# Second-half u made on ScalarE, channels paired per bank, and four mixing products taken channel by channel, at the end of a first feed-forward block

## The chip, the core and the metric

The kernel runs on one core of a Trainium2 chip. The core has a matrix engine (TensorE, PE in the profile; its weight loads are PEld), a vector engine (VectorE, DVE), an activation engine (ScalarE, ACT), GpSimd (POOL) and a queue engine that issues most transfers (SyncE, SP). Results of PE land in eight accumulator banks of PSUM, 2 KB per partition each, which DVE and ACT read; everything else lies in SBUF. The metric is the device time of one execution in microseconds; lower is better.

## The reference, cut to what matters

One transformer layer over 512 tokens of 1024 channels in float32: a modulated feed-forward block, a mixer of two branches (a chunked mLSTM and a forgetting attention), and a second feed-forward block.

```python
def hybrid_layer(x, c, ...):
    u = rms_norm(x, ffn1_norm_g) * (1 + sc1) + sh1
    x = x + 0.5 * g1 * swiglu(u, ffn1_w_in, ffn1_w_out)

    u = rms_norm(x, mix_norm_g) * (1 + sc2) + sh2        # the u of this text
    z = u @ w_mix + b_mix
    q_m, k_m, v_m, o_m, i_m, f_m, q_f, k_f, v_f, f_f, g_a, g_b = ...   # slices of z
    qk_m = silu(causal_conv(concatenate([q_m, k_m]), conv_w, conv_b))
    ...                                                   # mLSTM, attention, gates
    x = x + g2 * (merged @ w_out)
    u = rms_norm(x, ffn2_norm_g) * (1 + sc3) + sh3
    x = x + 0.5 * g3 * swiglu(u, ffn2_w_in, ffn2_w_out)
    return x
```

The change lies where `x` of the first block is complete, the second `u` is formed, and the first 512 columns of `z` (`q_m`, in four blocks of 128 columns) are computed.

## The kernel before, in words

Every float32 matrix product is made of three products of rounded parts. An operand `w` is split into a high part `wh` (ACT, line 96) and a remainder `wl` (DVE, line 98), and PE adds high by high (line 115), high by remainder and remainder by high (lines 116 and 117). Activations `u` are kept transposed: eight tiles of 128 channels by 512 tokens, each as a high part `uh[k]` and a remainder `ul[k]`.

`u_from` makes one channel tile for one half of the tokens (256 columns) out of a transposed piece in a bank: ACT writes `uh` (line 250: scale and shift in one pass), a second pass writes the unrounded `uf`, and a subtraction gives `ul` (line 255). The second pass is on DVE (line 254) unless `start` is set, in which case it is on ACT (line 252). The subtraction is on POOL for odd channels and on DVE for even ones; with `start` set, it is always on DVE.

`norm_turn` transposes the normalised tokens on PE (line 271) into four banks `b` and calls `u_from` for each channel. Before the change channel k and channel k + 4 share bank k % 4, and the sixteen transposes run through the channels in order, so a bank is complete only when its channel k + 4 is in.

In `run`, the first feed-forward block ends with `pair_out`. The first token half of `u` is made while that still runs. Then come the normalisation of the second half (`norm_scale`), the weights of the four `q_m` blocks (`ws`), the four products over the first 256 tokens into four banks `pp`, the transposes and `u` of the second half, and then the four products over the last 256 tokens (`gemm_stat`, block by block, each over its eight channels). After these follow the causal convolution of the four blocks (`qk_conv`), a narrow product for the gate columns (`gates`, 96 columns, weights `rawg`), and four more blocks, m = 4 to 7, which are `k_m`.

The order of the work is not just that of the text. The build places each engine's instructions in a list of its own, going by its own estimate of when inputs are ready, and then adds the waits between engines. In the kernel before it has mixed the products of the first two blocks with one another. Three kinds of buffer tie the places together:

- split weights `wh` and `wl`: four buffers each. The four `q_m` blocks hold all of them, so the gate weights can be split only when the first block's last product is done;
- raw weights `raw`: three buffers, in turn, the gate weights' `rawg` among them. The load for block 6 takes the buffer of `rawg` and waits for its split on DVE (line 98);
- banks `g`: four. The gate product takes the bank of the first `q_m` block, which ACT must have read (`cz`, line 956).

In `qk_conv` ACT copies the bank to `cz`, DVE does four multiply-adds into `cy` (lines 958 and 960), ACT applies silu (961) and rounds (964), and DVE takes the remainder `qkl` (965). In `gates` DVE adds the bias (`gz`, 922), ACT does three functions (923 to 925), for which it loads another function table twice, and DVE goes on (926 onward).

Of the kernel before, what the change touches and what calls it, by code (L numbers as in the profile page):

```python
# [20 lines left out]
P = 128  # L21
# [3 lines left out]
NK = 8  # L25
# [23 lines left out]
class Layer:  # L49
# [213 lines left out]
            self.u_tiles()  # L263
        return self.xnorm(hf, pool)

    def norm_turn(self, hf, xn, G, sh, b, ks=range(NK)):

        nc = self.nc
        for k in range(NK):
            for i in range(2):  # L270
                nc.tensor.transpose(b[k % 4][:, k // 4 * 256 + i * P:k // 4 * 256 + (i + 1) * P],
                                    xn[i][k // 4][:, k % 4 * P:(k % 4 + 1) * P], self.ident)
        u = lambda k: self.u_from(b[k % 4][:, k // 4 * 256:(k // 4 + 1) * 256], k, hf * 256, 256, G[:, k:k + 1], sh[:, k:k + 1], self.tp)
        for k in ks:
            u(k)
        return u

    def gemm_stat(self, ps, w, c0, c1, ks=range(NK)):
        wh, wl = w
        for k in ks:  # L280
            self.mm3(ps[:wh.shape[2], c0:c1], wh[:, k, :], wl[:, k, :],
                     self.uh[k][:, c0:c1], self.ul[k][:, c0:c1], k == 0, k == NK - 1)
# [178 lines left out]
    def product(self, ps, A, W, first, tail=0, hooks={}):  # L461

        chunks = [(c, min(2, NP - c)) for c in range(0, NP, 2)]
        def run(t, part, ops):
            ah, al, wh, wl = ops
            mm = self.nc.tensor.matmul
            c, n = part
            for k in range(n):
                s = slice(t * P, (t + 1) * P)
                a = (ah(c + k)[:, s], al(c + k)[:, s])  # L470
                end = c + k == NP - 1
                mm(ps[t], a[0], wh[:, k, :], start=first and c + k == 0, stop=False, skip_group_check=True)  # L472
                mm(ps[t], a[0], wl[:, k, :], start=False, stop=False, skip_group_check=True)  # L473
                mm(ps[t], a[1], wh[:, k, :], start=False, stop=end, skip_group_check=True)  # L474
        body, last = chunks[:len(chunks) - tail], chunks[len(chunks) - tail:]
        for i, part in enumerate(body):
            ops = (*A(*part), *W(*part))
            for t in range(2):
                run(t, part, ops)
            if i in hooks:  # L480
                hooks[i]()
        ops = [(*A(*part), *W(*part)) for part in last]
        for t in range(2):
            for part, o in zip(last, ops):
                run(t, part, o)
            yield t
# [809 lines left out]
    def run(self):  # L1296
        nc, tc, A = self.nc, self.tc, self.A
# [7 lines left out]
        with tc.tile_pool(name="f1t", bufs=1) as tp:  # L1305
            self.tp = tp
            self.consts(tp)
            with tc.tile_pool(name="st", bufs=1) as st:
                acc_ps = self.start(st, tp)
            with tc.tile_pool(name="f1h", bufs=1) as fp:  # L1310
                self.pair_tiles(fp)
                steps = self.ada_steps((2, 3, 4, 5), self.acc_pair(fp), self.gbank)
                w = self.three_blocks(A["ffn1_w_in"][0], A["ffn1_w_out"][0], acc_ps)
                self.ffn_pairs(A["ffn1_w_in"][0], A["ffn1_w_out"][0], 3, steps, 3, w)
                self.ss_tile()
                n2 = {}
                def scale():
                    n2["G"], n2["sh"] = self.mod_cols(3, gain(R_N2))
                    n2["xn"] = self.norm_scale(0, fp)
                def turn():  # L1320
                    n2["u"] = self.norm_turn(0, n2["xn"], n2["G"], n2["sh"],
                                             [self.tbank() for _ in range(2)] + [self.gbank() for _ in range(2)], ())
                def chans(i):
                    for k in (i, i + 4):
                        n2["u"](k)
                self.pair_out(A["ffn1_w_out"][0], 2, A["x"][0], False, {0: scale, 2: turn}, [lambda i=i: chans(i) for i in range(4)])
                xn = self.norm_scale(1, fp)
                ws = [self.w_stat(w_mix, m * P) for m in range(4)]
                pp = [self.gbank() for _ in range(4)]
                for m in range(4):  # L1330
                    self.gemm_stat(pp[m], ws[m], 0, 256)
                self.norm_turn(1, xn, n2["G"], n2["sh"], [self.tbank() for _ in range(4)])
            for tb in range(NT):
                for h in range(2):
                    nc.sync.dma_start(self.x_d[tb * P:(tb + 1) * P, h * 512:(h + 1) * 512], self.x[tb][h])
            for k in range(NK):
                self.dump(f"u2_{k}", self.uh[k].bitcast(F32))
# [5 lines left out]
        self.yb = [self.xp.tile([P, T], F32, name=f"yb{m}", tag=f"x{m}") for m in range(NK)]  # L1343
        self.qk = [None] * 8
        with tc.tile_pool(name="gates", bufs=1) as mp:
            for m in range(4):
                self.gemm_stat(pp[m], ws[m], 256, 512)
            for m in range(4):
                self.qk_conv(m, pp[m], yp, mp)
            columns = self.gates(mp, yp)  # L1350
            for m in range(4, 8):
                ps = self.gbank()
                self.gemm_stat(ps, self.w_stat(w_mix, m * P), 0, T)
                if m == 7:
                    with tc.issue_after(self.last_mm.ins):
                        columns()
                self.qk_conv(m, ps, yp, mp)
# [145 lines left out]
```

## Time and profile before

| what | value |
| --- | --- |
| median of 3 runs | 1333.47 us (1333.05 to 1334.53) |
| the profiled execution | 1333.42 us |
| its span, first to last instruction | 1331.6 us |
| PE busy | 1312.8 us, 99% of the span |
| DVE, ACT, POOL busy | 945.8, 631.3, 85.9 us |
| granted PE clock | 1.000 |
| `u` of the second half is subtracted | 397.04 to 401.9 us |
| products over the last 256 tokens | 396.07 to 409.35 us |

Times in the views are microseconds from the span's start; the second number of a row of the timeline is the time from the first start to the last end of the instructions merged in it, and a bracket names the idle time of the engine before it and what ended it. Matmuls overlap: one with 256 columns shows 0.28 us but the next starts 0.12 us after it.

### The profile page before, as it was taken

How to read it: one execution, taken by the hardware profiler on the slowest of the kernel's cores; microseconds unless marked ns; L12 is line 12 of the kernel's file. 1: busy time of each engine (PE TensorE's matmuls, PEld its weight loads, DVE VectorE, ACT ScalarE, POOL GpSimd, SP SyncE). 2: the span in 40 equal slices, each digit the busy share in tenths (PEclk: the TensorE clock that was granted, in tenths of full speed). 3: DMA queues.
4: the chain of work that ended last, by engine and by line, in shares of the span. 5: the costliest groups of instructions: out<-in, count | busy, mean ns of one | idle time of the engine just before them, and what ended most of it. 6: DMA issues, size and time to landing. Idle time of an engine off the chain costs nothing.

```text
span 1331.6 us, 17899 instructions
## 1 busy us (share of the span) xinstructions
PE 1312.8 (99%) x6468; PEld 1102.8 (83%) x6468; DVE 945.8 (71%) x1775; ACT 631.3 (47%) x1080; POOL 85.9 (6%) x140
## 2 busy tenths in 40 slices
PE   7999999999999999999999999999999999999998
PEld 6688888888888888988888878888888888888887
DVE  6777677688678867887685976777676565655655
ACT  5533433336557735566575686432354333433442
POOL 2000000001020000000000000002120000000000
PEclk9999999999999999999999999999999999999999
DMA  9776576777662434443343442787537555444474
GB/s 297 226 269 220 168 236 205 255 234 239 215 161 81 135 111 124 134 116 123 80 143 88 112 124 77 227 256 236 160 101 267 185 175 163 145 151 150 153 253 147
DMA packets 228621, 231.11 MB, mean 174 GB/s; under 512 B 12274, under 2 KB 183954, under 8 KB 228532
## 3 DMA queue, kind: packets, MB, share of 16 engines
q1 hardware_dynamic: 217428, 186.34, 46.4%
q0 software_dynamic: 11040, 43.61, 8.8%
q8 instruction: 51, 0.84, 0.2%
q14 instruction: 38, 0.31, 0.1%
q10 hardware_dynamic: 64, 0.02, 0.0%
HBM read 199.97 MB, written 29.95 MB: 173 GB/s over the span
## 4 chain that ended last, share of the span: by engine, by line
PE 91%; DVE 3%; ACT 2%; DMA 2%; issue 1%; SPq 0%; POOL 0%; ACTq 0%; DVEq 0%; POOLq 0%
PE g L117 21%; PE g L116 21%; PE g L115 21%; PE t L472 2%; PE t L474 2%; PE t L473 2%; PE t L1232 2%; PE t L446 1%; PE t L447 1%; PE t L445 1%; PE t L1202 1%; PE t L115 1%; PE t L117 1%; PE t L116 1%; PE g L829 1%
## 5 line engine op out<-in xcount | busy, mean ns | idle before, releaser
L96 ACT ACTIVATE wh<-raw 128x1024 fp32r<-128x1024 f32 x218 | 226.5, 1043 | 387.6 <-PE g L116 97.4
L116 PE MATMUL g<-ul,wh 128*128 128x512 f32 (+2 forms) x984 | 369.9, 376 | 1.1 <-DVE ul L255 0.8
L115 PE MATMUL g<-uh,wh 128*128 128x512 f32 (+2 forms) x984 | 370.1, 377 | 0.1
L117 PE MATMUL g<-uh,wl 128*128 128x512 f32 (+2 forms) x984 | 369.4, 376 | 0.2 <-DVE wl L98 0.2
L98 DVE TENSOR_TENSOR wl<-raw,wh 128x1024 fp32r<-128x1024 f32 x218 | 263.4, 1211 | 141.5 <-ACT wh L96 130.1
L116 PEld LDWEIGHTS g<-ul,wh 128*128 128x128 f32 (+1 forms) x984 | 185.0, 188 | 34.7 <-DVE ul L255 1.0
L117 PEld LDWEIGHTS g<-uh,wl 128*128 128x128 f32 (+1 forms) x984 | 184.9, 188 | 34.0 <-DVE wl L98 0.4
L115 PEld LDWEIGHTS g<-uh,wh 128*128 128x128 f32 (+1 forms) x984 | 184.7, 188 | 34.2 <-ACT sl L368 0.5
L115 PE MATMUL g<-wh,uh 128*128 128x512 f32 (+1 forms) x320 | 111.9, 350 | 0.0
L116 PE MATMUL g<-wl,uh 128*128 128x512 f32 (+1 forms) x320 | 111.0, 347 | 0.0
L117 PE MATMUL g<-wh,ul 128*128 128x512 f32 (+1 forms) x320 | 111.0, 347 | 0.0
L296 DVE SCALAR_TENSOR_TENSOR acc<-raw,ccol,acc 128x1024 f32<-128x1024 f32 (+1 forms) x63 | 66.0, 1065 | 43.0 <-DMA raw<-in_w_ada_dram 42.7
L117 PEld LDWEIGHTS g<-wh,ul 128*128 128x128 f32 x320 | 60.5, 189 | 7.8
L115 PEld LDWEIGHTS g<-wh,uh 128*128 128x128 f32 x320 | 60.5, 189 | 7.7 <-DVE tk L1085 0.5
L116 PEld LDWEIGHTS g<-wl,uh 128*128 128x128 f32 x320 | 60.5, 189 | 7.3
L369 DVE TENSOR_TENSOR hp<-g,sl 128x512 f32<-128x512 f32 x43 | 29.5, 689 | 51.6 <-PE g L117 50.8
L116 PE MATMUL g<-yl,wh 128*128 128x512 f32 x128 | 49.8, 389 | 0.0
L115 PE MATMUL g<-yl,wh 128*128 128x512 f32 x128 | 49.8, 389 | 0.0
L117 PE MATMUL g<-yl,wl 128*128 128x512 f32 x128 | 49.8, 389 | 0.0
L422 ACT ACTIVATE wh<-rw 128x1024 fp32r<-128x1024 f32 x22 | 23.3, 1058 | 49.0 <-issue 31.5
L1184 ACT ACTIVATE S<-S,mn 128x128 f32<-128x128 f32 (+1 forms) x64 | 35.5, 556 | 16.0 <-DVE mn L1176 8.9
L1446 POOL TENSOR_TENSOR sg<-sg,ta 128x512 f32<-128x512 f32 x8 | 13.6, 1694 | 452.4 <-DMA raw<-in_w_branch_b_dram 421.2
(339 smaller groups left out, 2252.1 us busy)
## 6 DMA issues: line engine op xcount, KB each, us to landing
raw<-in_ffn_w_in_dram SPq DMA_DIRECT2D x82, 512.0 KB, 4.7
raw<-in_w_ada_dram SPq DMA_DIRECT2D x56, 512.0 KB, 4.3
raw<-in_w_mix_dram SPq DMA_DIRECT2D x48, 512.0 KB, 3.9
rw<-in_ffn_w_out_dram POOLq DMA_DIRECT2D x20, 1024.0 KB, 6.8
S_d<-rw POOLq DMA_DIRECT2D x22, 768.0 KB, 4.0
raw<-S_d SPq DMA_DIRECT2D x30, 512.0 KB, 3.6
raw<-in_w_mix_dram SPq DMA_DIRECT2D x32, 256.0 KB, 3.9
ar<-in_w_ada_dram SPq DMA_DIRECT2D x14, 512.0 KB, 7.6
```

The lines of the kernel that those rows point to most:

```text
L96: self.last_hi = nc.scalar.activation(hi, src, AF.Copy)
L98: self.last_lo = self.last_wl = (eng or nc.vector).tensor_tensor(lo, src, hi, op=SUB)
L115: mm(ps, lh, rh, start=start, stop=False)
L116: mm(ps, lh, rl, start=False, stop=False)
L117: self.last_mm = mm(ps, ll, rh, start=False, stop=stop)
L296: nc.vector.scalar_tensor_tensor(a, r[:, cut(i)], self.ccol[:, k:k + 1], a, op0=MUL, op1=ADD)
L369: nc.vector.tensor_tensor(h, ps_b[:, c0:c1], s[:, :c1 - c0], op=MUL)
L472: mm(ps[t], a[0], wh[:, k, :], start=first and c + k == 0, stop=False, skip_group_check=True)
L473: mm(ps[t], a[0], wl[:, k, :], start=False, stop=False, skip_group_check=True)
L474: mm(ps[t], a[1], wh[:, k, :], start=False, stop=end, skip_group_check=True)
L1184: nc.scalar.activation(S[:, ws], S[:, ws], AF.Exp, scale=-1.0, bias=m, accum_out=sm[:, qb:qb + 1])
L1232: nc.tensor.matmul(po[:, q0:], vt[pr][:, kb, i % 2, :], Px[:, o:o + T - q0], start=n == 1, stop=n == 8)
```

## The change

Three things change, all for the second token half of this `u` only; the other calls of `norm_turn` keep the old form.

- `norm_turn` gets `act`. With it, channels 2j and 2j + 1 share bank j, and `u_from` is called with `start` set: `uf` comes from ACT (line 252) rather than DVE, and all eight subtractions are on DVE rather than four on POOL.
- The four products over the last 256 tokens are written channel by channel for channels 0 to 5 (new function `gemms`: for each channel, the four blocks), and block by block for channels 6 and 7.
- Nothing else in the text changes; the lines behind move down by 8 or 9.

```diff
-    def norm_turn(self, hf, xn, G, sh, b, ks=range(NK)):
+    def norm_turn(self, hf, xn, G, sh, b, ks=range(NK), act=False):
 
         nc = self.nc
+        place = (lambda k: (b[k // 2], k % 2 * 256)) if act else (lambda k: (b[k % 4], k // 4 * 256))
         for k in range(NK):
+            ps, c = place(k)
             for i in range(2):
-                nc.tensor.transpose(b[k % 4][:, k // 4 * 256 + i * P:k // 4 * 256 + (i + 1) * P],
-                                    xn[i][k // 4][:, k % 4 * P:(k % 4 + 1) * P], self.ident)
-        u = lambda k: self.u_from(b[k % 4][:, k // 4 * 256:(k // 4 + 1) * 256], k, hf * 256, 256, G[:, k:k + 1], sh[:, k:k + 1], self.tp)
+                nc.tensor.transpose(ps[:, c + i * P:c + (i + 1) * P], xn[i][k // 4][:, k % 4 * P:(k % 4 + 1) * P], self.ident)
+        def u(k):
+            ps, c = place(k)
+            self.u_from(ps[:, c:c + 256], k, hf * 256, 256, G[:, k:k + 1], sh[:, k:k + 1], self.tp, act)
         for k in ks:
             u(k)
         return u
+
+    def gemms(self, ps, ws, c0, c1, ks=range(NK)):
+        for k in ks:
+            for p, w in zip(ps, ws):
+                self.gemm_stat(p, w, c0, c1, (k,))
...
-                self.norm_turn(1, xn, n2["G"], n2["sh"], [self.tbank() for _ in range(4)])
+                self.norm_turn(1, xn, n2["G"], n2["sh"], [self.tbank() for _ in range(4)], act=True)
...
+            self.gemms(pp, ws, 256, 512, range(6))
             for m in range(4):
-                self.gemm_stat(pp[m], ws[m], 256, 512)
+                self.gemm_stat(pp[m], ws[m], 256, 512, (6, 7))
```

What this does to the engines' lists is seen at three places. In the names, `uh_2955` to `uh_2962` and `ul_2963` to `ul_2970` are channels 0 to 7; `g_3295` to `g_3298` are the banks of the four `q_m` blocks, with weights `wh_3273`/`wl_3274`, 3279/3280, 3285/3286 and 3291/3292; `t_3395` to `t_3398` are the banks of the transposes.

The first place is PE at the start of the products over the last 256 tokens. Before:

```order
L115 MATMUL g_3295<-uh_2955,wh_3273 128x256
L115 MATMUL g_3296<-uh_2955,wh_3279 128x256
L115 MATMUL g_3297<-uh_2955,wh_3285 128x256
L115 MATMUL g_3298<-uh_2955,wh_3291 128x256
L116 MATMUL g_3295<-ul_2963,wh_3273 128x256
L117 MATMUL g_3295<-uh_2955,wl_3274 128x256
L115 MATMUL g_3295<-uh_2956,wh_3273 128x256
L116 MATMUL g_3295<-ul_2964,wh_3273 128x256
L117 MATMUL g_3295<-uh_2956,wl_3274 128x256
```

And with the change:

```order
L115 MATMUL g_3295<-uh_2955,wh_3273 128x256
L116 MATMUL g_3295<-ul_2963,wh_3273 128x256
L117 MATMUL g_3295<-uh_2955,wl_3274 128x256
L115 MATMUL g_3296<-uh_2955,wh_3279 128x256
L116 MATMUL g_3296<-ul_2963,wh_3279 128x256
L117 MATMUL g_3296<-uh_2955,wl_3280 128x256
L115 MATMUL g_3297<-uh_2955,wh_3285 128x256
L116 MATMUL g_3297<-ul_2963,wh_3285 128x256
L117 MATMUL g_3297<-uh_2955,wl_3286 128x256
L115 MATMUL g_3298<-uh_2955,wh_3291 128x256
L116 MATMUL g_3298<-ul_2963,wh_3291 128x256
L117 MATMUL g_3298<-uh_2955,wl_3292 128x256
```

The remainder of channel 1, `ul_2964`, is the operand of the eighth product before and of the fourteenth now; that of channel 0 moves from the fifth place to the second. The first two blocks' last products stood 53 and 47 places ahead of the gate product's first, and stand 19 and 13 places ahead of it now.

The second place is ACT, where it makes `u`. Before, the eight `uh` stand alone, one bank after another:

```order
L250 ACTIVATE uh_2955<-t_3395,sh_2951,G_2952 128x256
L250 ACTIVATE uh_2956<-t_3396,sh_2951,G_2952 128x256
L250 ACTIVATE uh_2957<-t_3397,sh_2951,G_2952 128x256
L250 ACTIVATE uh_2958<-t_3398,sh_2951,G_2952 128x256
L250 ACTIVATE uh_2959<-t_3395,sh_2951,G_2952 128x256
```

With the change `uh` and `uf` of a channel follow one another, sixteen instructions in all, and two channels come out of each bank:

```order
L252 ACTIVATE uf_3415<-t_3395,sh_2951,G_2952 128x256
L250 ACTIVATE uh_2956<-t_3395,sh_2951,G_2952 128x256
L252 ACTIVATE uf_3419<-t_3395,sh_2951,G_2952 128x256
L250 ACTIVATE uh_2957<-t_3396,sh_2951,G_2952 128x256
L252 ACTIVATE uf_3423<-t_3396,sh_2951,G_2952 128x256
L250 ACTIVATE uh_2958<-t_3396,sh_2951,G_2952 128x256
```

The third place is DVE after that, at the remainders of the weights of block 4 (`wl_3683`), block 5 (`wl_3727`) and block 6 (`wl_3771`). Before, block 6's stands three places behind block 5's:

```order
L98 TENSOR_TENSOR wl_3683<-raw_3680,wh_3682 128x1024
L98 TENSOR_TENSOR wl_3727<-raw_3724,wh_3726 128x1024
L965 TENSOR_TENSOR qkl_3577<-cy_3568,qkh_3576 128x512
L958 TENSOR_SCALAR cy_3594<-cz_3593,colA 128x512
L98 TENSOR_TENSOR wl_3771<-raw_3768,wh_3770 128x1024
```

With the change the list after block 5's reads:

```order
L973 TENSOR_TENSOR qkl_3577<-cy_3568,qkh_3576 128x512
L930 TENSOR_SCALAR gz<-g_3624,gbias 96x512
L973 TENSOR_TENSOR qkl_3590<-cy_3581,qkh_3589 128x512
L966 TENSOR_SCALAR cy_3594<-cz_3593,colA 128x512
L966 TENSOR_SCALAR cy_3607<-cz_3606,colA 128x512
L968 SCALAR_TENSOR_TENSOR cy_3594<-cz_3593,colA,cy_3594 128x512
...
L968 SCALAR_TENSOR_TENSOR cy_3607<-cz_3606,colA,cy_3607 128x512
L934 SCALAR_TENSOR_TENSOR gl<-gz,gl 96x512
L98 TENSOR_TENSOR wl_3771<-raw_3768,wh_3770 128x1024
```

Between them stand six multiply-adds in all. Block 6's remainder has moved behind the convolution of two more blocks and behind `gl`, the gate value that comes back from ACT. On ACT its high part now stands ahead of the first silu:

```order
L96 ACTIVATE wh_3682<-raw_3680 128x1024
L96 ACTIVATE wh_3726<-raw_3724 128x1024
L96 ACTIVATE wh_3770<-raw_3768 128x1024
L969 ACTIVATE cy_3568<-cy_3568 128x512
L964 ACTIVATE cz_3593<-g_3297,colA 128x512
L972 ACTIVATE qkh_3576<-cy_3568 128x512
L969 ACTIVATE cy_3581<-cy_3581 128x512
```

Before, it stood behind all of these and the fourth `cz`.

## The prediction

> **What bounds the kernel now.** I read the page's busy shares and its chain of waits first. The chain's shares by engine are its fourth part.
>
> ```profile
> span 1331.6 us, 17899 instructions
> PE 1312.8 (99%) x6468; PEld 1102.8 (83%) x6468; DVE 945.8 (71%) x1775; ACT 631.3 (47%) x1080; POOL 85.9 (6%) x140
> PE 91%; DVE 3%; ACT 2%; DMA 2%; issue 1%; SPq 0%; POOL 0%; ACTq 0%; DVEq 0%; POOLq 0%
> ```
>
> PE is the bound nearly everywhere, so only idle PE time can be won, and work given to ACT or DVE costs nothing until PE waits for it. Next I read PE's waits between 360 and 460 us, and then PE's timeline at the place of the change.
>
> ```profile
> PE g L116 <- DVE ul L255: 0.8, 1, 0.8
> PE g L116 <- POOL ul L255: 0.3, 1, 0.3
> ```
>
> ```profile
> 394.17 1.91 PE L271 MATMUL t<-ident,xn 128*128 128x128 f32 x16
> 396.07 0.74 PE L115 MATMUL g<-uh,wh 128*128 128x256 f32 x4
> 397.64 0.39 PE L116 MATMUL g<-ul,wh 128*128 128x256 f32 x1 [0.83 <-DVE ul L255]
> 397.86 0.28 PE L117 MATMUL g<-uh,wl 128*128 128x256 f32 x1
> 397.98 0.28 PE L115 MATMUL g<-uh,wh 128*128 128x256 f32 x1
> 398.57 0.39 PE L116 MATMUL g<-ul,wh 128*128 128x256 f32 x1 [0.31 <-POOL ul L255]
> ...
> 409.35 0.39 PE L115 MATMUL g<-uh,wh 128*96 128x512 f32 x1
> 409.58 0.39 PE L116 MATMUL g<-ul,wh 128*96 128x512 f32 x1
> 409.81 0.40 PE L117 MATMUL g<-uh,wl 128*96 128x512 f32 x1
> ...
> 414.91 0.39 PE L115 MATMUL g<-uh,wh 128*128 128x512 f32 x1
> ...
> 425.81 0.39 PE L115 MATMUL g<-uh,wh 128*128 128x512 f32 x1
> ```
>
> Sixteen transposes, then the 96 products over the last 256 tokens from 396.07, then the gate product at 409.35, block 4 at 414.91 and block 6 at 425.81. Undisturbed products start 0.12 us apart (397.86, 397.98), so 96 take 11.52. They take 409.35 − 396.07 = 13.28. The loss is **1.76 us**: 1.14 in the two waits shown, the rest in slower starts around them (0.22 from 397.64 to the next, not 0.12). That is all there is to win in these products.
>
> ACT and DVE show why PE waits, and what comes after:
>
> ```profile
> 395.46 3.76 ACT L250 ACTIVATE uh<-t,sh,G 128x256 fp32r<-128x256 f32 x8 [2.12 <-PE t L271]
> 403.19 0.84 ACT L96 ACTIVATE wh<-rawg 128x768 fp32r<-128x768 f32 x1 [3.97 <-PE g L116]
> 403.94 1.25 ACT L956 ACTIVATE cz<-g,colA 128x512 f32<-128x512 f32 x2
> ```
>
> ```profile
> 396.13 1.00 DVE L254 TENSOR_SCALAR uf<-t,G,sh 128x256 f32<-128x256 f32 x2 [3.24 <-ACT uh L250]
> 397.04 0.55 DVE L255 TENSOR_TENSOR ul<-uf,uh 128x256 fp32r<-128x256 f32 x1
> 404.06 0.96 DVE L98 TENSOR_TENSOR wl<-rawg,wh 128x768 fp32r<-128x768 f32 x1 [1.80 <-ACT wh L96]
> 404.94 1.00 DVE L958 TENSOR_SCALAR cy<-cz,colA 128x512 f32<-128x512 f32 x2
> 405.85 4.06 DVE L960 SCALAR_TENSOR_TENSOR cy<-cz,colA,cy 128x512 f32<-128x512 f32 x6
> 409.83 2.35 DVE L98 TENSOR_TENSOR wl<-raw,wh 128x1024 fp32r<-128x1024 f32 x2
> ```
>
> DVE reads a bank only after ACT has read it, makes two `uf`, and only then the first `ul` at 397.04. POOL's first comes later still, and DVE's last is done at 401.3, after which it idles:
>
> ```profile
> 400.90 0.41 DVE L255 TENSOR_TENSOR ul<-uf,uh 128x256 fp32r<-128x256 f32 x1
> ```
>
> ```profile
> 397.78 1.64 POOL L255 TENSOR_TENSOR ul<-uf,uh 128x256 fp32r<-128x256 f32 x2
> ```
>
> **The transposes.** They start 0.11 us apart (16 in 1.91, the last one's own length taken off). ACT's first `uh` waits for the tenth, since channel 4 shares channel 0's bank. Paired, the bank is complete after the fourth: six fewer, 0.66 earlier, 394.80. PE itself is then free for the first product a little before 396.07, where it had just waited for `uh` (395.46 + 0.55); I take 395.95. Gain 0.12.
>
> **`u` from ACT.** Eight `uh` in 3.76 are 0.46 each with 0.55 for the last. The trace has no `uf` on ACT in this stage; its lower bound is the same 0.46 (same input, same size), its upper the 0.62 that 128x512 pieces cost here (two `cz` in 1.25). I take 0.46, from the row with this shape. So `uf_0` runs from 395.26 to 395.81. `ul_0` on DVE then costs 0.41 to 0.55 (the two rows) and is there at 396.3 to 396.4. PE wants it at 396.07: a wait of 0.33 remains, plus 0.10 for the slower start, **0.45** with the handover. With `uf` at 0.62 it is 0.6.
>
> From there a channel costs ACT 0.92 and DVE 0.42, while PE spends 12 × 0.12 = 1.44 on it. `ul_1` is ready at 397.3 and wanted at 398.0; each further channel adds 0.5 of slack. The order by channel is what gives this cover: in the old order `ul_2964` would be wanted at the eighth product, 0.7 sooner. The eight `uf` taken off DVE and four `ul` off POOL cost nothing: both stand idle there. ACT's extra eight lie in its idle 3.97 before 403.19.
>
> So the gate product starts at 395.95 + 11.52 + 0.45 = 407.92 in place of 409.35. **Term one: −1.43**; bounds −1.88 (no wait at all) and −1.2 (dear `uf`, long `ul`).
>
> **What moves later.** Ordering by channel ends all four blocks late, so the buffers of the first come free late. The gate weights' high part waited for the first block's last high product and started at 403.19. This product now stands 20 places ahead of the gate product: 407.92 − 2.40 + 0.28 = 405.80. ACT 405.85 to 406.69; DVE's remainder from 406.72, against 404.06, **2.66 later**, until 407.68. PE wants it with its third gate product, 407.92 + 0.46 = 408.38: margin 0.7. The bank it needs is copied by `cz` 0.75 after the split starts, 406.60 to 407.28, before 407.92: margin 0.6. Cost 0.
>
> Block 4's remainder: from the gate's to it DVE works without a pause, 409.83 − 404.06 = 5.77, so 412.49 + 1.22 = 413.71. PE wants it 0.46 after block 4 begins, 414.91 − 1.43 + 0.46 = 413.94. **Margin 0.23**; before it was 4.3. I cost it at 0, and 0.5 as the other end.
>
> Block 6's remainder has moved behind the gate bias on DVE and, through `gl`, behind two function table loads on ACT. Its load, its steps on ACT and DVE, and the gate's functions before:
>
> ```profile
> 405.05 17.52 SPq L85 DMA_DIRECT2D raw<-in_w_mix_dram  x5
> ```
>
> ```profile
> DMA to landing us min/median/max: 3.9/4.1/4.3
> ```
>
> ```profile
> 412.10 0.68 DVE L965 TENSOR_TENSOR qkl<-cy,qkh 128x512 fp32r<-128x512 f32 x1
> ...
> 413.36 1.22 DVE L98 TENSOR_TENSOR wl<-raw,wh 128x1024 fp32r<-128x1024 f32 x1
> ...
> 418.87 0.74 DVE L922 TENSOR_SCALAR gz<-g,gbias 96x512 f32<-96x512 f32 x1
> ```
>
> ```profile
> 412.00 1.05 ACT L96 ACTIVATE wh<-raw 128x1024 fp32r<-128x1024 f32 x1
> ...
> 419.64 0.63 ACT L923 ACTIVATE ge<-gz 96x512 f32<-96x512 f32 x1
> 420.29 1.28 ACT L924 ACT_TABLE_LOAD   x1
> 421.59 0.63 ACT L924 ACTIVATE ge<-ge 96x512 f32<-96x512 f32 x1
> ```
>
> The load takes `rawg`'s buffer, now free at 407.7 rather than 405.05, and lands 4.1 later, 411.8. ACT, in its order, then does that split (about 1.0), a silu, a `cz` and a rounding (0.55 to 0.6 each) to 414.5. The first `qkl` on DVE waits for that rounding and is due at 406.72 + 5.77 + 2.28 = 414.77. DVE then does `qkl` 0.6, `gz` 0.7 to 416.1, another `qkl`, which ACT's second rounding lets start at 416.25, two `cy` (0.9) and six multiply-adds (4.0), until 421.7. ACT meanwhile goes on from 416.2: first function 0.6, table 1.3, second 0.6, block 7's split 1.0, table 1.3, third 0.6, until 421.6. So `gl` starts at 421.7 (0.6) and the remainder of block 6 ends at 422.3 + 1.22, about 423.6. PE wants it at 425.81 − 1.43 + 0.46 = 424.84: **margin 1.2**. Before, DVE had it at 414.6. Cost 0; if the two chains run a few tenths slow at each step, 1.0 is the other end.
>
> Block 7's follows one scan and one split (2.3) behind and is wanted 5.5 behind: no cost.
>
> The four transposition banks, the buffers of `uf` and the number of products do not change. Behind block 7 the lists are as before but for a few neighbours, so PE's time there is taken over whole.
>
> One rule of the Trainium skill speaks against the change: "ScalarE: Activation LUTs", section on what ACT_TABLE_LOAD costs, gives a switch about 2.66 us in all, with a drain of 1.38 behind the load. The row above shows the next function 1.30 after the load's start, so this trace has no such drain here, and the sum goes by the row. By the page's figure `gl` would come 2.7 later; an estimate by it has PE wait 1.5 for block 6 and the time end at 1333.5.
>
> **The sum.** Term one −1.43, three margins at 0. The profiled execution would go from 1333.42 (1331.6 span and 1.8 around it) to 1331.99. The median shown is 0.05 above the profiled one, hence **1332.0 us**. A measurement of this kernel tells about 0.2%, 2.7 us, from no change, so this counts as no change.
>
> **Rivals.**
>
> *Given back at block 6.* Each of the two table loads between `gz` and `gl` holds ACT for twice the 1.3 of the row. PE then waits 2 × 1.3 − 1.2 = 1.4, and the time is that of before, 1333.4. For it: the margin is new, and DVE and ACT hand work to each other four times within it. Against it: the row, in which the next function starts at once. Chance 0.13, in which the smaller slips at blocks 4 and 6 are counted. It is the case that the page on table loads would make; the row is against that figure.
>
> *Slower: ACT stuck behind the load for block 6.* ACT's list now has this split ahead of the first silu. Before, the load had landed at 409.2, 2.8 us before ACT took it at 412.0; now ACT stands and waits for it, with silu, two `cz`, the rounding and so `gz` behind it. Up to 0.27 late costs nothing; then each microsecond moves `gl` and block 6's remainder one for one. From 1.5 late (5.6 us to land) PE waits; from 2.9 late, at 7.0, the whole gain is lost. With the slowest 512 KB row of the page,
>
> ```profile
> ar<-in_w_ada_dram SPq DMA_DIRECT2D x14, 512.0 KB, 7.6
> ```
>
> it is 3.5 late, PE waits 2.0, and the time is 1334.0. Against it: loads land within 3.9 to 4.3 in this stretch. Chance 0.11, half of it beyond 0.2%, where the loads behind it come late too.
>
> *The change does not do it.* `ul_0` may need all transposes still, if the wait is placed on a later one. Then `uh_0` starts at 396.1, `ul_0` is ready at 397.7 and PE waits 1.6: 1333.5. The list shows four transposes into the first bank, so 0.04.
>
> *More than forecast.* Only 1.88 is to be had here; over 2.7 needs luck elsewhere. 0.07.
>
> **Chances.** Forecast, −1.0 to −1.9, 0.65; the rivals as above. Faster by over 0.2% 0.07; within 0.87; slower by over 0.2% 0.06. Range: from 1331.1 (the −1.88 bound and half a microsecond of scatter, the three runs shown spreading 1.5) to 1333.9 (all given back, and scatter). The slow rival's tail and the lucky one lie outside.
>
> **What would show it.** PE's waits for `ul` at 0.3 to 0.4 once, none from POOL; the first `uh` at about 394.8; gate product at about 407.9; ACT waiting 1.9 to 2.3 for block 6's load; `wl` of block 4 just before its third product; `wl` of block 6 done near 423.6. A PE wait for `wl` at line 98 near 414 or 425 proves me wrong on the margins. A gate product after 408.5 proves me wrong on `u`.

## The result, and the profile after

The changed kernel takes 1331.95 us (median of 22 runs, 1330.63 to 1333.46); the kernel before, beside it, 1333.59 us (22 runs, 1332.63 to 1334.90). The ratio is 0.9987, with a 95% interval of 0.9981 to 0.9993. That is 1.64 us less, against 1.4 to 1.5 forecast, and it lies within 0.2% of no change.

The profiled execution of the changed kernel is the fastest of its 22 (1330.63 us). Its busy shares answer to those shown of before:

```profile
span 1328.8 us, 17898 instructions
PE 1311.5 (99%) x6468; PEld 1102.8 (83%) x6468; DVE 942.9 (71%) x1771; ACT 633.0 (48%) x1087; POOL 82.1 (6%) x136
```

Four DVE instructions fewer (eight `uf` gone, four `ul` come), four POOL instructions fewer, eight ACTIVATEs more and one table load fewer, so seven more on ACT: the edit did what its text says. The span is 2.8 shorter, and 1.24 of that has nothing to do with the change: the first of the sixteen transposes starts at 392.93 rather than 394.17. Over the kernels of this study that start lies anywhere from 392.93 to 395.34 us, although the change touches nothing ahead of it. So times from the span's start cannot be compared, and I read lengths instead, on PE's timeline, from the first transpose of the second half:

- **A**: to the first gate product (128x96, 512 columns);
- **B**: to the first value product, which follows block 7 and the four transposes of the gate columns (`t<-ident,ggm`);
- **C**: to the end of the span.

| kernel | first transpose | A | B | C |
| --- | --- | --- | --- | --- |
| before | 394.17 | 15.18 | 43.00 | 937.43 |
| changed | 392.93 | 13.66 | 41.49 | 935.87 |
| difference | | −1.52 | −1.51 | −1.56 |

The whole gain is made in A, and all of it is still there at B. At the end it is there too, as far as C can show, which repeats to 0.4 only (the first experiment). PE's timeline of the changed kernel at the main places that the prediction quoted of before, and where B ends:

```profile
392.93 1.91 PE L273 MATMUL t<-ident,xn 128*128 128x128 f32 x16
394.59 0.36 PE L115 MATMUL g<-uh,wh 128*128 128x256 f32 x1
395.10 0.39 PE L116 MATMUL g<-ul,wh 128*128 128x256 f32 x1
395.32 0.28 PE L117 MATMUL g<-uh,wl 128*128 128x256 f32 x1
...
406.59 0.39 PE L115 MATMUL g<-uh,wh 128*96 128x512 f32 x1
...
412.61 0.39 PE L117 MATMUL g<-uh,wl 128*128 128x512 f32 x1
...
423.52 0.39 PE L117 MATMUL g<-uh,wl 128*128 128x512 f32 x1
...
434.04 0.46 PE L953 MATMUL t<-ident,ggm 64*128 64x64 f32 x4
434.42 0.50 PE L115 MATMUL g<-wh,uh 128*128 128x512 f32 x1
```

The first product now starts 1.66 after the first transpose, directly behind the last one, where it was 1.90 (396.07 − 394.17). The 96 products take 406.59 − 394.59 = 12.00 where 96 at 0.12 are 11.52, so 0.48 of the old 1.76 is left. It sits in one place: the second product, the first with `ul`, starts 0.51 after the first instead of 0.12, and the third 0.22 after that. The list of PE's waits for 380 to 470 us has no row any more. The wait has moved to the row of that product's weight load, which stands under an engine name of its own:

```profile
395.10 0.19 PEld L116 LDWEIGHTS g<-ul,wh 128*128 128x128 f32 x1 [0.34 <-DVE ul L255]
```

ACT, and then DVE, at the same places:

```profile
393.57 0.56 ACT L250 ACTIVATE uh<-t,sh,G 128x256 fp32r<-128x256 f32 x1 [1.92 <-PE t L273]
394.03 0.56 ACT L252 ACTIVATE uf<-t,sh,G 128x256 f32<-128x256 f32 x1
...
404.56 0.85 ACT L96 ACTIVATE wh<-rawg 128x768 fp32r<-128x768 f32 x1 [3.60 <-issue]
405.31 1.25 ACT L964 ACTIVATE cz<-g,colA 128x512 f32<-128x512 f32 x2
...
410.31 1.06 ACT L96 ACTIVATE wh<-raw 128x1024 fp32r<-128x1024 f32 x1 [1.85 <-DMA raw<-in_w_mix_dram]
...
414.85 0.63 ACT L931 ACTIVATE ge<-gz 96x512 f32<-96x512 f32 x1 [0.25 <-DVE gz L930]
415.50 1.28 ACT L932 ACT_TABLE_LOAD   x1
416.80 0.63 ACT L932 ACTIVATE ge<-ge 96x512 f32<-96x512 f32 x1
...
429.65 0.63 ACT L943 ACTIVATE ggm<-gfs 4x512 f32<-4x512 f32 x1
```

```profile
394.62 0.43 DVE L255 TENSOR_TENSOR ul<-uf,uh 128x256 fp32r<-128x256 f32 x1 [3.42 <-ACT uf L252]
...
405.44 0.96 DVE L98 TENSOR_TENSOR wl<-rawg,wh 128x768 fp32r<-128x768 f32 x1 [3.57 <-ACT wh L96]
...
411.20 2.35 DVE L98 TENSOR_TENSOR wl<-raw,wh 128x1024 fp32r<-128x1024 f32 x2
...
414.08 0.74 DVE L930 TENSOR_SCALAR gz<-g,gbias 96x512 f32<-96x512 f32 x1
...
420.97 1.22 DVE L98 TENSOR_TENSOR wl<-raw,wh 128x1024 fp32r<-128x1024 f32 x1
```

`ul_0` starts at 394.62 and is done at 395.05, and PE takes it at 395.10. The four late buffers are all in time: the gate remainder at 406.40, wanted with the third gate product at 407.05 (406.59 + 0.46); the gate's bank copied at 405.31 + 0.68 = 405.99, wanted at 406.59; block 4's remainder at 411.20 + 1.22 = 412.42, wanted at 412.61; block 6's at 422.19, wanted at 423.52.

### The profile page after: what moved, and what is told of

Read it like the earlier page. It is cut to its first block, busy times and chain, and to the rows that moved or that the text cites. A ratio compares the mean times of both kernels' runs of the same rounds, so it can differ in the third digit from the quotient of the medians.

```text
span 1328.8 us, 17898 instructions
## 1 busy us (share of the span) xinstructions
PE 1311.5 (99%) x6468; PEld 1102.8 (83%) x6468; DVE 942.9 (71%) x1771; ACT 633.0 (48%) x1087; POOL 82.1 (6%) x136
## 4 chain that ended last, share of the span: by engine, by line
PE 94%; ACT 2%; DVE 2%; DMA 1%; issue 1%; ACTq 0%; SPq 0%; DVEq 0%
PE g L117 22%; PE g L116 22%; PE g L115 22%; PE t L480 2%; PE t L481 2%; PE t L482 2%; PE t L1240 2%; PE t L454 2%; PE t L453 2%; PE t L455 2%; PE g L837 1%; PE t L1210 1%; PE t L115 1%; PE t L117 1%; PE t L116 1%; PE t L1181 1%
```

## The experiments

Two theories stood against each other. The prediction's: PE lost its time to a late `u`; ScalarE, the pairs and the order by channel each take part of that away, the order giving the cover for the remainders, and the buffers that come late keep small margins. The rival: the build's own list mixes the blocks anyway, so the order by channel adds nothing to the supply of `u`, and nothing to the time. Four of the kernels below (the changed one once more, ScalarE and pairs alone, all eight channels by channel, the remainder of channel 0 wanted later) were timed together, 11 runs each, with the kernel before at 1333.23 us in 33. The others were timed once each with their trace, and for these the lengths A and B decide.

### The changed kernel once more

> The changed kernel itself, as the yardstick of this group. Three lengths are read on PE's timeline, which the scatter of the start-up does not touch. A: from the first of the sixteen transposes to the first gate product (before 409.35 - 394.17 = 15.18, changed 13.66). B: from the same transpose to the first value product after block 7 (before 437.17 - 394.17 = 43.00, changed 41.49). C: to the end of the span (before 937.4, changed 935.9). Expected again: A 13.7, B 41.5, C 935.9 within 0.3, and a time 1.4 to 1.6 below the kernel before.

1331.69 us, ratio 0.9988 (0.9979 to 0.9997); A 13.65, B 41.48, C 936.23. The lengths A and B repeat to 0.01, C to 0.4.

### ScalarE and pairs alone, products block by block

```diff
-            self.gemms(pp, ws, 256, 512, range(6))
             for m in range(4):
-                self.gemm_stat(pp[m], ws[m], 256, 512, (6, 7))
+                self.gemm_stat(pp[m], ws[m], 256, 512)
```

> u from ScalarE and the channels in pairs, but the four products written block by block as before. Theory 1 (the prediction's): the order by channel gives the cover; without it the remainders are wanted about 0.7 sooner, PE waits for ul again, A is 14.3 to 14.4 and half the gain is gone. Theory 2: with u supplied every 0.92 us any mixed order finds its remainders ready, only the first one waits, and A is 13.7, B 41.5 and the time that of the changed kernel; the list of this build takes three blocks in turn, 9 products or 1.08 us to a channel, still slower than 0.92.

A is 13.70, the changed kernel's to 0.04: the order by channel does next to nothing for A. But the time is 1332.56 us, ratio 0.9996 (0.9987 to 1.0005), 0.9 above the changed kernel beside it, and B is 42.13, longer by 0.65. Neither theory had that. PE's waits for 380 to 470 us, and PE, ACT and GpSimd at the place:

```profile
PE t L953 <- POOL cz L963: 0.6, 1, 0.6
```

```profile
434.79 0.39 PE L117 MATMUL g<-uh,wl 128*128 128x512 f32 x1
435.74 0.43 PE L953 MATMUL t<-ident,ggm 64*128 64x64 f32 x4 [0.56 <-POOL cz L963]
436.10 0.50 PE L115 MATMUL g<-wh,uh 128*128 128x512 f32 x1
```

```profile
433.72 1.28 ACT L943 ACT_TABLE_LOAD   x1
435.01 0.63 ACT L943 ACTIVATE ggm<-gfs 4x512 f32<-4x512 f32 x1
```

```profile
435.53 0.10 POOL L963 MEMSET cz<- 128x3 f32 x1 [8.22 <-DVE cy L968]
```

The list of waits names GpSimd's clearing of three columns of `cz`, which the gate columns do not read. It ended at 435.63, and ACT's last gate function, which they do read, at 435.64. The two cannot be told apart by their ends. If it is the gate function, the wait is there because the gate chain has stayed late while PE came 1.5 sooner: `gz` is added at 419.15 here,

```profile
419.15 0.74 DVE L930 TENSOR_SCALAR gz<-g,gbias 96x512 f32<-96x512 f32 x1
```

25.18 after the first transpose, where it is 24.70 before (418.87) and 21.15 in the changed kernel (414.08). That reading called for a run of its own, and a control.

### The same with the gate chain shortened

```diff
-        nc.scalar.activation(gm[32:36, :], fs, AF.Exp, scale=-1.0)
+        nc.scalar.activation(gm[32:36, :], fs, AF.Copy, scale=-1.0)
```

> The run with ScalarE's u alone, block by block, with one thing more: the third function of the gates (the exponential of line 943, whose table load and the load back behind it go with it) is a plain scaled copy, so the values of the gate columns are not the reference's. It asks what PE waited 0.6 us for at the gate columns' transposes. If it is the gate chain on ScalarE (the third function was done at 435.64 there, PE's transposes began at 435.74, while PE's last product before them began at 434.79 and needs about 0.3 to the next), the function is done 1.28 earlier, about 40.4 after the first transpose where PE wants it at about 41.1, and the wait goes whole: first transpose to first value product 41.5 in place of 42.13. If it is GpSimd's clearing of three columns of cz, as the list of waits names it, nothing has changed for that and the wait stays at 0.4 to 0.6: 41.9 to 42.1. If it is the order of the products themselves, 42.1 too. First transpose to gate product stays 13.7 by all three.

A 13.70, B 41.53, and no wait is left. ACT, PE and GpSimd at the place:

```profile
433.72 0.63 ACT L943 ACTIVATE ggm<-gfs 4x512 f32<-4x512 f32 x1
```

```profile
434.78 0.39 PE L117 MATMUL g<-uh,wl 128*128 128x512 f32 x1
435.10 0.46 PE L953 MATMUL t<-ident,ggm 64*128 64x64 f32 x4
```

```profile
435.52 0.10 POOL L963 MEMSET cz<- 128x3 f32 x1 [8.21 <-DVE cy L968]
```

The function now starts at 433.72, where its table load started, and is done at 434.35, 1.29 sooner. PE goes at 435.10, before GpSimd's clearing at 435.52, which has not moved. So the releaser that the trace named was wrong; PE had waited for the gate function. The time, taken once, is 1331.61 us beside 1333.48.

### The control: the changed kernel with the gate chain shortened

The same edit on the changed kernel.

> The changed kernel with the same edit (the third gate function a scaled copy without its table load, so the gate columns' values are not the reference's): the control. In the changed kernel this function was done at 430.28, 3.8 before PE's transposes at 434.04, so with the gate chain as the cause nothing moves: first transpose to gate product 13.66, to first value product 41.5. If the edit itself speeds PE up in this stretch by another way, 41.2 or less, and the run before it would prove nothing.

A 13.66, B 41.51: nothing moves (1332.24 us, once). In the changed kernel the chain has 3.8 us to spare: `ggm` is done at 430.28, PE's transposes start at 434.04. The edit makes PE no faster by itself.

### All eight channels by channel

```diff
-            self.gemms(pp, ws, 256, 512, range(6))
-            for m in range(4):
-                self.gemm_stat(pp[m], ws[m], 256, 512, (6, 7))
+            self.gemms(pp, ws, 256, 512)
```

> All eight channels channel by channel, so the first block's last high product stands 11 places ahead of the gate product and not 20: 1.08 us later. Measured margins in the changed kernel: the bank of the first block is copied at 405.99 and wanted at 406.59 (0.60), the gate remainder is there at 406.40 and wanted at 407.05 (0.65), block 4's at 412.42 and wanted at 412.61 (0.19). If late buffers decide (the prediction's margins): the gate product waits 0.5, A 14.15, block 4 or 5 waits again 0.4 to 0.8, B 42.4 to 42.8, and the time is 0.9 to 1.3 above the changed kernel. If margins of a few tenths are of no account: A 13.7, B 41.5, no difference.

1332.71 us, ratio 0.9995 (0.9986 to 1.0004), 1.0 above the changed kernel beside it; A 14.19, B 42.52. Here the late buffers do decide. PE's waits, its timeline, its weight loads and ACT:

```profile
PE g L115 <- ACT cz L964: 0.4, 1, 0.4
```

```profile
407.18 0.28 PE L115 MATMUL g<-uh,wh 128*128 128x256 f32 x1
...
408.07 0.47 PE L115 MATMUL g<-uh,wh 128*96 128x512 f32 x1 [0.36 <-ACT cz L964]
408.38 0.39 PE L116 MATMUL g<-ul,wh 128*96 128x512 f32 x1
408.60 0.40 PE L117 MATMUL g<-uh,wl 128*96 128x512 f32 x1
...
413.94 0.39 PE L116 MATMUL g<-ul,wh 128*128 128x512 f32 x1
414.47 0.50 PE L115 MATMUL g<-uh,wh 128*128 128x512 f32 x1
414.81 0.39 PE L116 MATMUL g<-ul,wh 128*128 128x512 f32 x1
```

```profile
408.48 0.16 PEld L117 LDWEIGHTS g<-uh,wl 128*96 128x96 f32 x1 [0.17 <-DVE wl L98]
...
414.47 0.19 PEld L115 LDWEIGHTS g<-uh,wh 128*128 128x128 f32 x1 [0.57 <-ACT cz L964]
```

```profile
406.59 0.85 ACT L96 ACTIVATE wh<-rawg 128x768 fp32r<-128x768 f32 x1 [4.68 <-issue]
407.34 1.25 ACT L964 ACTIVATE cz<-g,colA 128x512 f32<-128x512 f32 x2
...
413.75 0.67 ACT L964 ACTIVATE cz<-g,colA 128x512 f32<-128x512 f32 x1
```

All blocks now end at the very end of the 96. ACT's gate split starts 12.71 after the first transpose (11.63 in the changed kernel), the copy of the first bank behind it at 407.34, and the gate product waits for that copy until 408.07, 0.53 later than three products behind 407.18 would have put it. The second loss is 0.41: the product at 414.47 comes 0.53 behind the one before it and its own successor 0.34, where 0.23 each is the rule. It is the first of block 5, which the build has moved up between block 4's second and third; it takes a bank whose copy ended at 413.75 + 0.67 = 414.42. The list of waits has only the first of the two. Between the two lies a loss of 0.08, the slower second product behind the first wait (408.38, 0.31 after 408.07). The gate's third product loads its weights late, at 408.48 behind `wl`, but starts 0.22 behind the second, so this remainder costs nothing. The losses are two banks. Block 4's remainder was no sooner there than the second of them: it ended at 414.46 (413.24 + 1.22), and in the changed kernel's order PE would have wanted it at 414.17 (413.94 + 0.23). That PE would have waited for it there is worked out, not run. Leaving two channels by block is not a detail: the first blocks' banks must be copied a little before the last products.

### Four channels by channel, four by block

```diff
-            self.gemms(pp, ws, 256, 512, range(6))
+            self.gemms(pp, ws, 256, 512, range(4))
             for m in range(4):
-                self.gemm_stat(pp[m], ws[m], 256, 512, (6, 7))
+                self.gemm_stat(pp[m], ws[m], 256, 512, range(4, 8))
```

> Four channels channel by channel and four block by block. The first block ends 24 products sooner than in the changed kernel, so each margin of the later buffers grows by well over 1 us. A 13.7 and B 41.5 as in the changed kernel: margins that are not used up cost nothing. If the small margins of the changed kernel cost it anything that its trace does not show, B is shorter here by that much.

A 13.65, B 41.48: those of the changed kernel (1332.85 us, once; its first transpose stood at 395.10). The first block ends 18 products sooner, not the 24 expected: ACT's gate split starts 9.46 after the first transpose (404.56), 2.17 earlier than in the changed kernel. The buffers come free sooner and nothing is won: margins of 0.2 to 1.3 that are kept cost nothing.

### The order alone; pairs without ScalarE; ScalarE without pairs

Three kernels keep the order by channel and take back one part of the way in which `u` is made, or both:

```diff
-                self.norm_turn(1, xn, n2["G"], n2["sh"], [self.tbank() for _ in range(4)], act=True)
+                self.norm_turn(1, xn, n2["G"], n2["sh"], [self.tbank() for _ in range(4)])
```

> Only the order of the four products changed; u as before (second pass on DVE, every other subtraction on POOL, channels four apart in a bank). A (first transpose to first gate product): before 15.18, changed 13.66. By the rows of before, ul of channel 0 is ready at 397.59 and now wanted at the fifth product, 396.55: one wait of 1.05 and 0.10 behind it, and POOL's ul of channel 1 (398.5) is wanted at the fourteenth, 398.8, so its wait of 0.31 goes. A 14.5 to 14.7. If the order were the main thing, A would be near 13.9.

```diff
-            self.u_from(ps[:, c:c + 256], k, hf * 256, 256, G[:, k:k + 1], sh[:, k:k + 1], self.tp, act)
+            self.u_from(ps[:, c:c + 256], k, hf * 256, 256, G[:, k:k + 1], sh[:, k:k + 1], self.tp)
```

> Channels in pairs per bank and the order by channel, but the second pass stays on DVE and every other subtraction on POOL. The first u can start after four transposes (0.66 sooner), but ACT and DVE have to take turns at a bank that holds neighbouring channels. Theory: the pairs are worth the first 0.5 or so and the hand-overs take part of it back: A 14.0 to 14.3, with a second wait of 0.4 for POOL's ul of channel 1. If pairing alone made the gain: A 13.7.

```diff
-        place = (lambda k: (b[k // 2], k % 2 * 256)) if act else (lambda k: (b[k % 4], k // 4 * 256))
+        place = lambda k: (b[k % 4], k // 4 * 256)
```

> The second pass on ScalarE and the order by channel, but channels k and k + 4 in a bank as before, so the first u waits for ten transposes. uh of channel 0 from 395.46, uf from 395.92 to 396.47, ul at 396.95, wanted at the fifth product 396.55: one wait of 0.4 and 0.10 behind it, and the first product at 396.07 rather than 395.8. A 13.9 to 14.0: ScalarE is worth more than the pairs. If the pairs are worth their whole 0.66: A 14.3.

| kernel | A | against before | B | time, once |
| --- | --- | --- | --- | --- |
| order alone | 14.60 | −0.58 | 42.44 | 1332.88 |
| order, pairs | 14.14 | −1.04 | 41.99 | 1331.93 |
| order, ScalarE | 13.96 | −1.22 | 41.79 | 1333.31 |
| all three (changed) | 13.66 | −1.52 | 41.49 | 1331.69 (11 runs) |
| ScalarE and pairs, no order | 13.70 | −1.48 | 42.13 | 1332.56 (11 runs) |

All three A lie within what was expected of them. The parts do not add up. The order alone takes 0.58 from A, since with the old `u` the supply is short and the order moves the second `ul` back; with ScalarE and pairs it takes 0.04. ScalarE is worth 0.48 on top of order and pairs (14.14 to 13.66), the pairs 0.30 on top of order and ScalarE (13.96 to 13.66). Beside it the single times show why lengths were read: the slowest of the three by time has the shortest A of the three, because its first transpose started at 395.34.

### The remainder of channel 0 wanted later

In the changed kernel PE's second product wants `ul_0`. For channel 0 alone the twelve products are put in another order: the four high by high, the four with the weights' remainder, and then the four with `ul_0`.

```diff
+        mm = self.nc.tensor.matmul
         for k in ks:
+            if not k:
+                hi, lo = self.uh[0][:, c0:c1], self.ul[0][:, c0:c1]
+                for p, w in zip(ps, ws):
+                    mm(p[:, c0:c1], w[0][:, 0, :], hi, start=True, stop=False)
+                for p, w in zip(ps, ws):
+                    mm(p[:, c0:c1], w[1][:, 0, :], hi, start=False, stop=False)
+                for p, w in zip(ps, ws):
+                    mm(p[:, c0:c1], w[0][:, 0, :], lo, start=False, stop=False)
+                continue
             for p, w in zip(ps, ws):
                 self.gemm_stat(p, w, c0, c1, (k,))
```

> The changed kernel with channel 0 taken in another order: first the eight products of its high part for the four blocks, then the four of its remainder, so ul of channel 0 is wanted at the ninth product and not the second, 0.84 us later. The one wait that the change leaves is 0.39 plus 0.10 for the slower start. Theory: it goes whole, A 13.2, B 41.0, the time 0.4 to 0.5 below the changed kernel. Rival: PE is then held by the first high parts (uh of channel 0 or 1), or the margins of the gate and block 4 (0.60, 0.65, 0.19) shrink because the later buffers are wanted 0.45 sooner: then A 13.2, but B stays at 41.3 to 41.5. The buffers' release moves by the same 0.45, so I expect the first.

1331.12 us, ratio 0.9985 (0.9976 to 0.9994); A 13.25, B 41.09, each 0.4 shorter than in the changed kernel. PE's timeline (the lines below the edit have moved by ten):

```profile
395.30 1.91 PE L273 MATMUL t<-ident,xn 128*128 128x128 f32 x16
396.97 0.72 PE L287 MATMUL g<-uh,wh 128*128 128x256 f32 x4
397.52 0.64 PE L289 MATMUL g<-uh,wl 128*128 128x256 f32 x4
398.00 0.64 PE L291 MATMUL g<-ul,wh 128*128 128x256 f32 x4
...
408.55 0.39 PE L115 MATMUL g<-uh,wh 128*96 128x512 f32 x1
```

The 96 products take 408.55 − 396.97 = 11.58 of a least 11.52. The wait for `ul_0` is gone whole, and with it what there was to win in this stage. By lengths this is the best kernel of the study, ahead of both; by times it is ahead of the kernel before, while its lead over the changed kernel (0.6 in the medians) is smaller than their intervals.

Not tried: the rival of a late load for block 6. No run delays this load alone.

## Why the prediction was right or wrong

**Term one: right.** −1.43 was forecast for A and −1.52 measured. By its steps: "six fewer, 0.66 earlier" put the first `uh` at 394.80, 0.63 after the first transpose, and it came 0.64 after (393.57). The gain at the handover was sized at 0.12 and measured 0.24: PE goes on straight behind the sixteenth transpose, with no gap at all. "A wait of 0.33 remains, plus 0.10 for the slower start" measured 0.39 and 0.10. `ul_0` was there as forecast, 2.12 after the first transpose (2.13 to 2.23 worked out); PE was there sooner, so more of the same lateness shows as a wait. `uf` on ACT at the lower bound, 0.46 each, measured 0.45 from start to start. The run with the remainder wanted later goes just past the bound: with no wait for `ul_0` at all A is 1.93 shorter than before, against −1.88, which had the handover at 0.12. One reading of before was off without harm. A bracket counts only from the end of the earlier record (0.83 from 396.07 + 0.74 = 396.81 to 397.64), so 1.14 was too little for the two waits. By starts they are 1.09 (397.64 against 396.07 + 4 × 0.12 = 396.55) and 0.47 (398.57 against 397.98 + 0.12 = 398.10), and the slower starts take 0.20 of the 1.76.

**"The order by channel is what gives this cover": wrong.** This step failed. Without the order A is 13.70, only 0.04 longer. The argument looked at the eighth product of the old list, where `ul_2964` would be wanted at 397.3 (0.7 before 398.0), just when it is ready, so that nothing would cover it. But that list was laid out for the old supply of `u`; with a faster supply the build lays out another. There `ul_2964` is the operand of the tenth product, which starts at 397.21, and DVE has it at 397.00 (396.58 + 0.42). Only where `u` stays slow does the order help A, by 0.58.

**"PE's time behind block 7 is taken over whole": true here, but for a reason that the prediction did not have.** That the whole gain stayed is, in this step, luck. The prediction priced four late buffers and left out a fifth thing that PE waits for in this stretch: `ggm`, the last function of the gate chain, at the transposes behind block 7. The row that should have been read stands in the trace of before:

```profile
435.55 0.63 ACT L935 ACTIVATE ggm<-gfs 4x512 f32<-4x512 f32 x1
...
436.79 0.46 PE L945 MATMUL t<-ident,ggm 64*128 64x64 f32 x4
437.17 0.50 PE L115 MATMUL g<-wh,uh 128*128 128x512 f32 x1
```

That is a margin of 0.61 (436.79 − 436.18) ahead of a PE that was to come 1.4 sooner. With the gate chain where it was, about 0.8 of the gain would have been given back, and in the run without the order by channel 0.61 is (A 1.48 shorter than before, B 0.87). The changed kernel escapes because its DVE list has `gz` 3.55 sooner from the first transpose, which the prediction's own rows on block 6 show ("`gz` 0.7 to 416.1", against 419.61 before, 418.87 + 0.74) without following it to `ggm`. From `gz` on the chain is another 1.11 shorter, with one table load fewer in it, so `ggm` is done 37.35 after the first transpose, against 42.01 before. The order by channel earns its keep there, and not in the supply of `u`: all the kernels with it have `gz` 19.7 to 22.0 after the first transpose and no wait for `ggm`, the two without it that keep the whole gate chain 24.7 and 25.2. Why the build takes `gz` sooner with this order is not shown by any run.

**The margins: right, one by one.** Gate remainder 0.7 forecast, 0.65 measured; gate bank 0.6 and 0.60; block 4's remainder 0.23 and 0.19; block 6's 1.2 and 1.33. ACT waited 1.85 for block 6's load, just under the 1.9 to 2.3. The run with all eight channels by channel shows that the first two are real: move the ends of the blocks back by nine products, and the gate's bank costs 0.53, while the gate's remainder comes only just in time. No run shows a wait for the remainder of block 4 or of block 6.

**The rivals.** *Given back at block 6* did not come: ACT's next function starts 1.30 after the table load (415.50, 416.80), as before. By the row 1.3 of margin is left there; the Trainium skill's page "ScalarE: Activation LUTs", section on what ACT_TABLE_LOAD costs, gives a drain of 1.38 with each load. No row here shows one, behind the load or ahead of it: the function ahead ends at 415.48 (414.85 + 0.63). *ACT stuck behind the load* had its place (the 1.85 in ACT's row) but not its price: the load was no later than its kind, since ACT goes at 410.31 and the queue had issued the load at 406.42, 3.9 earlier. *The change does not do it* falls with the first `uh`. *More than forecast* did not come either.

**The sum.** 1332.0 was forecast from a profiled execution 0.05 from the median shown. The 22 runs give 1331.95, but the kernel before also measures 0.12 higher beside them, so 1.64 is the difference in medians and 1.56 that in the length C, each about 0.1 to 0.2 above term one.

## What to carry to other kernels

When an edit brings the bounding engine forward, list everything that this engine waits for over the next two hundred or so of its products, and not only the buffers that the edit moves: the input with the least margin in the old trace, 0.61 here, is what can take the gain. Measure a small edit by lengths between fixed instructions of the bounding engine, from the first one that the edit touches; they repeat to 0.01 where whole times of one kernel spread by 1.5 to 2.8 us. Where an operand comes late, order the products so that those without it go first: eight products moved ahead of the four with `ul_0` brought 0.4 us here.

## What the runs showed of the hardware that was not expected

The releaser named in a list of waits can be a bystander. GpSimd's clearing ended 0.01 before ACT's function and was named for a wait of 0.56; a run in which only ACT's function moved took the wait away while the clearing stood where it was.

A wait of PE can be missing from PE's list of waits. In the changed kernel the product with `ul_0` starts 0.39 late, with eight channels by channel that of block 5 0.30 late, and neither row has a bracket; the rows of their weight loads have (0.34 and 0.57). The earlier product still shows as running for part of that time (until 394.95 and 414.33); the 0.15 and 0.14 that are left have no bracket either. Gaps between starts show both.

ACT's sixteen passes for `u` start 0.45 us apart throughout, yet their records grow, from 0.56 for the first to 0.65 for the last. What the longer records stand for no run here shows; DVE's `ul` follow 0.91 apart, so nothing behind them is later for it.
